# Splitting an output projection into three steps of rows, and joining a short projection, in a hybrid trunk step

## The chip, the cores and the metric

The kernel runs on one core of a Trainium2 chip. The metric is device time in microseconds (us) of that core, the median over several runs. A core has five engines that work side by side: TensorE (PE in the profile; its weight loads are shown apart as PEld), VectorE (DVE), ScalarE (ACT), GpSimd (POOL) and SyncE (SP), which here issues all the DMAs. SBUF is the on-chip memory with 128 partitions, PSUM the small memory into which TensorE writes its results.

## What is computed

One inference step of a layer for 2048 prompt tokens and 128 decode tokens ("samples": 8 sequences of 16 tokens). One input projection feeds three groups of heads, and one output projection joins them:

```python
h = rms_norm(x, norm_g) @ w_in                    # 1024 -> 3654 columns
fox_cols, rwkv_cols, mem_cols = jnp.split(h, ...)
# 6 "fox" heads x 64: causal attention with forget gates (bias on the logits)
# 6 RWKV-7 heads x 64: token shift, decay and learning rate from a small LoRA, a state scan
# 4 memory heads x 64: attention into 256 memory tokens
o = jnp.concatenate([o_f * silu(g_f), o_r * silu(g_r), o_m * silu(g_m)], axis=-1)   # 1024 rows
y = x + o @ w_out
```

For the samples the fox heads attend to 512 cached keys each, the memory heads to 256 cached ones. The mixed row `o` has 1024 entries, which the kernel treats as eight chunks of 128: chunks 0, 1, 2 are the fox heads in pairs, 3, 4, 5 the RWKV heads, 6, 7 the memory heads. The output projection is a sum over these chunks, so it can be made in steps, each adding its chunks to a partial `y`.

## The kernel before

**Two phases.** The first (lines 122 to 943) makes the projections and the RWKV heads, in four rounds of 512 tokens; round 0 carries the 128 sample tokens as well, so it has 640. The second (from 946) makes the fox and memory attention and the output projection. What passes between them goes through DRAM: `q_d`, `k_d`, `v_d`, `mq_d` (token by column), the gates `fg_d`, `mg_d`, the mixed rows `o_d` (column by token), and the partial result `y_d`.

**Projections.** A weight block of up to 256 columns is split into a high and a low part by `wd_load` (line 177), and a product is three matmuls (high x high, high x low, low x high) for each of eight chunks of the 1024 inputs, 24 matmuls in all. `proj_d` (210) gives columns by tokens: the weight is stationary and up to 512 tokens stream. `wide` (735) gives tokens by columns: a tile of 128 tokens is stationary and 256 columns stream, so no transposition is needed for `q`, `k`, `v` and the memory queries. At the head of a round `lora_in` (328) makes 64 LoRA columns and 6 forget-gate columns in one `proj_d` of 70 columns; `forget_cols` (316) turns the 6 back into tokens by columns. The second 128 columns of the memory queries ("m", 128) come out of `pair` (772) and `narrow` (748) as columns by tokens, are copied, and are turned by `turn` (756).

**Attention.** A unit is one pair of heads and one block of 512 queries: 12 fox units (three pairs, four blocks) and 8 memory units. For every tile of 128 keys (`kt`) and each head, `scores` (1144) makes two matmuls into `pS`, ACT makes the exponentials `P` (1153), and the running sum `z` of the exponentials is added up at 1159 and 1161. `ZE = "GGV"` says on which engine: every third key tile from 2 on is VectorE's, the others GpSimd's. `values` (1163) multiplies with the values, four key tiles behind. `sums` (1199) and `out` (1218) scale the result by the reciprocal sums, which come through DRAM, and by the gate, and write it to `o_d`; the fox unit that comes last keeps its result in SBUF. The samples have steps of their own (`sample`, 1226): three pairs of fox heads, two of memory heads.

**Output projection.** `project` (1348) takes a set of chunks and a tile of 128 tokens: it loads the rows of `o_d`, splits them (`oh`, ACT and GpSimd), loads the partial `y` (`xo`, two buffers), makes three matmuls into `py` per chunk and half, adds on VectorE and writes. The weights `W` lie in buffers of the tag `big`, of which there are seven; the samples and the memory heads use the same ones.

**The order.** Every step is put at a place between 0 and 1 on the way through the 12 fox units (`spread`, 1454; the units go with their lengths). The memory units and the first step of the projection (chunks 3, 4, 5, all 17 tiles, onto `x`) lie from 0.02 to 0.35; all samples from 0.35 to 0.6, fox first; then, to 0.8, chunks 6, 7 for tiles 12 to 15, the weights of chunks 0, 1, 2, and the sample tile. Tiles 0 to 11 get chunks 6, 7, 0, 1, 2 in one step (`late`, 1440), four behind each of the last fox units, from 0.8 on. Tiles 12 to 15 get chunks 0, 1 from 0.98 on, and chunk 2 at the very end (`project_last`, 1378). After that `_arrange` (1924) plans all instructions anew: it lists them by engine with costs of its own, ranks them by the place in which they were written and by what lies behind them, and gives each engine one fixed order. So the places are wishes, and the queues are in the order that the plan gives.

Of the kernel before, what the change touches and what calls it, by code (L numbers as in the profile page):

```python
# [30 lines left out]
X0, X3, X1, X2 = 0.02, 0.35, 0.6, 0.8  # L31
# [19 lines left out]
def kernel(ctx: ExitStack, tc: tile.TileContext, I: dict, O: dict):  # L51
# [70 lines left out]
    with ExitStack() as p1:  # L122
# [166 lines left out]
        def shifted(hl, c, m, ci, xk, blocks, it, key, extra=0, tok0=0):  # L289
# [5 lines left out]
            for off, n in blocks:  # L295
                out = proj_d(hl, c, m + extra, xk, off, n)
                if extra:
                    forget_cols(out[64:70, :n], spans(tok0, off, n))
# [17 lines left out]
        def forget_cols(src, where):  # L316
            n = sum(x[1] for x in where)
            sb = sm.tile([128, 512], F32, tag="gth", name="fsb")[64:70, :n]
            S.copy(sb, src)
            pt = pj.tile([128, 512], F32, tag="pj", name="pf")  # L320
            for t in range(n // 128):
                PE.transpose(pt[:, 6 * t:6 * t + 6], sb[:, 128 * t:128 * t + 128], ident[64:70, 64:70])
            for a, m, r0 in where:
                t0, t1, nt = a // 128, r0 // 128, m // 128
                tt(V, fl[:, t1:t1 + nt, :], pt[:, 6 * t0:6 * (t0 + nt)].rearrange("p (t h) -> p t h", h=6),
                   bf_b.unsqueeze(1).to_broadcast([128, nt, 6]), A_)

        def lora_in(hl, xk, blocks, it, tok0):
            xs, xss = shifted(hl, 0, 64, 12, xk, blocks, it, "l", 6, tok0)
# [344 lines left out]
        turned = []  # L674

        def after(*step):

            if turned:
                f, *args = turned.pop()
                f(*args)  # L680
            if step:
                turned.append(step)


# [50 lines left out]
        def wide(parts, xk, nt, t0):  # L735
            hl = wd_load(*columns(parts), src="w_mem" if parts[0][0] in "KV" else "w_in")
            for a in range(0, nt, 2):
                m = min(2, nt - a)
                out = pj.tile([128, 2, 256], F32, tag="pj", name="pjt")
                for t in range(m):  # L740
                    ts_ = slice(128 * (a + t), 128 * (a + t) + 128)
                    for k in range(KC):
                        for x, y in ((0, 0), (0, 1), (1, 0)):
                            mm(out[:, t], xk[k][:, x, ts_], hl[y][k // 4][:, k % 4],
                               start=k == 0 and x + y == 0, stop=k == KC - 1 and x == 1)
                put(out[:, :m], parts, 16 if a == 4 else t0 + a)

        def narrow(hl, c, part, xk, blocks, tok0):

            for off, nb in blocks:  # L750
                out = proj_d(hl, c, 128, xk, off, nb)
                sb = sm.tile([128, 512], F32, tag="gth", name="tsb")[:, :nb]
                S.copy(sb, out[:, :nb])
                after(turn, sb, off, nb, part, tok0)

        def turn(sb, off, nb, part, tok0):
            pt = pj.tile([128, 512], F32, tag="pj", name="ptok")
            for t in range(nb // 128):
                PE.transpose(pt[:, 128 * t:128 * t + 128], sb[:, 128 * t:128 * t + 128], ident)
            for a, m, r0 in spans(tok0, off, nb):  # L760
                put(pt[:, a:a + m].rearrange("p (t c) -> p t c", c=128), [part], r0 // 128)
# [10 lines left out]
        def pair(xk, blocks, tok0, *two):  # L772

            at = lambda w, c: {"f": FG, "g": MG, "m": MQ}[w] + c
            hl = wd_load(*((at(w, c), 128) for w, c in two))
            for j, (w, c) in enumerate(two):
                if w == "m":
                    narrow(hl, 128 * j, (w, c), xk, blocks, tok0)
                else:
                    gate(hl, 128 * j, (fg_d if w == "f" else mg_d)[c:c + 128], xk, blocks, tok0)  # L780

        def constants():
# [3 lines left out]
            ts(V, qg8, qg8, 0.125, None, M, ALU.bypass)  # L786
            mg, mG = (x.rearrange("p a b -> p (a b)") for x in (maskG, I["maskG"]))
# [98 lines left out]
        for it in range(4):  # L886
# [10 lines left out]
            nt, t0 = n // 128, 4 * it  # L897
# [4 lines left out]
                (("m", 128), ("f", 0)), (("f", 128), ("f", 256)), (("g", 0), ("g", 128)))]  # L902
            for p in range(3):
                finish()
                cols = {}
                for two in ((("k", RW + 384, 3), ("r", RW, 0)), (("v", RW + 768, 6), ("g", RG, 9))):
                    hl = wd_load(*((c0 + 128 * p, 128) for _, c0, _ in two))
                    for j, (key, _, ci) in enumerate(two):
                        cols[key] = shifted(hl, 128 * j, 128, ci + p, xk, blocks, it, key)
# [23 lines left out]
        after()  # L933
# [12 lines left out]
    with ExitStack() as p2:  # L946
# [15 lines left out]
        gap = lt.tile([128, 112], F32, tag="gap", name="gap", bufs=1)  # L962
        V.memset(gap[0:1, 0:1], 0.0)
# [174 lines left out]
        def attend(U, q, qb, hp, fox, gsrc, dst):  # L1138
# [79 lines left out]
            def out():  # L1218
                tt(V, R["ob"], R["ob"], R["rb"], M)
# [6 lines left out]
        def sample(fox, hp):  # L1226
# [6 lines left out]
            def load():  # L1233
                m = big("sC")
# [18 lines left out]
            def masked(h):  # L1253
                rr = slice(64 * h, 64 * h + 64)
                D = R["D", h] = big("sD")
# [6 lines left out]
                m = big("sA")[:, 0:512 * nkt]  # L1262
# [6 lines left out]
            def soft(h):  # L1269
# [4 lines left out]
                sb = R["sb"] = R["D", h][:, 640:1280]  # L1274
# [20 lines left out]
            def turn(h):  # L1295
                PT = R["PT", h] = R["D", h][:, 1280:1920].rearrange("p (a b) -> p a b", b=128)
# [51 lines left out]
        def project(W, ks, t, xsrc, dst):  # L1348
# [3 lines left out]
            def load():  # L1352
                ot = lt.tile([128, 5, 128], F32, tag="ot", name="ot", bufs=1)[:, :n]
# [6 lines left out]
                W["o", t] = oh = lt.tile([128, 2, 5, 128], F32R, tag="oh", name="oh")[:, :, :n]  # L1360
# [17 lines left out]
        def project_last(W, held):  # L1378
# [9 lines left out]
            def rows_in(t):  # L1388
                ot = lt.tile([128, 5, 128], F32, tag="ot", name="ot", bufs=1)[:, 0:2]
                ts_ = slice(1536 + 128 * t, 1664 + 128 * t)  # L1390
                SY.dma_start(ot, o_d[0:256, ts_].rearrange("(k p) t -> p k t", p=128))
                ohs[t] = oh = lt.tile([128, 2, 5, 128], F32R, tag="oh", name="oh")[:, :, 0:2]
# [3 lines left out]
            def split():  # L1396
                ohs["held"] = hl = lt.tile([128, 2, 5, 128], F32R, tag="oh", name="oh")[:, :, 0:4]
                src = held["ob"].rearrange("p (t c) -> p t c", t=4)
                S.copy(hl[:, 0], src)
                tt(V, hl[:, 1], src, hl[:, 0].bitcast(F32), SUB)  # L1400

            def half(t, j, last):
                y, js = ys[t // 2][:, t % 2], slice(512 * j, 512 * j + 512)
                oh, own, ks = (ohs["held"], t, (2,)) if last else (ohs[t], 0, (0, 1))
                py = qa.tile([128, 512], F32, tag="pt", bufs=PTB, name="py")
                for k in ks:
                    for a, b in ((0, 0), (0, 1), (1, 0)):
                        mm(py, oh[:, a, own if last else k, :], W[k][:, b, js],
# [646 lines left out]
```

## Time and profile before

| | |
|---|---|
| median of 3 runs | 1762.91 us (1760.62 to 1770.31) |
| profiled execution, its own time | 1764.2 us |
| its span, first to last instruction | 1762.2 us |
| mean granted TensorE clock | 0.971 |
| busy: PE, DVE, ACT, POOL | 1639.0, 1053.2, 727.2, 677.6 us |
| moved by DMA | 302.88 MB, 172 GB/s over the span |

In the profile a row of a group names the line, the engine, the operation, what is written and what is read (buffer numbers left out), the shape and the count, then busy time and mean length of one, then the idle time ahead of them and what ended it. Almost all matmuls share line 58 and almost all tensor operations line 61 (they are helpers), so the tile names tell them apart: `pjd` and `pjt` are projections, `pS` scores, `pm` the products for the row maximum, `po` values, `py` the output projection, `sA` to `sD` the samples' buffers. Some matmul records can be missing from a trace.

### The profile page before, as it was taken

The page shows a single profiled execution, that of the slowest core. Times are in us where ns is not written, and L with a number is a line of the kernel's source. Part 1 is how long each engine was busy: PE and PEld are TensorE (multiplying, and loading weights), DVE is VectorE, ACT ScalarE, POOL GpSimd, SP SyncE. Part 2 cuts the span into 40 slices and gives each one's busy share as a digit, 9 for nine tenths or more (in the row PEclk, how much of TensorE's full clock was granted, in tenths as well). Part 3 has the DMA queues.
Part 4 walks back from the last instruction along what each step waited for, and adds up shares of the span by engine and source line. Part 5 has one row for each costly group of instructions (what it writes and reads, how often), then busy time and mean ns, then how long its engine had stood idle before and what let it go on. Part 6 is the DMA issues. An engine that isn't in the chain of part 4 may idle for free. (4 is left out here: it accounts for less than half of the span.)

```text
span 1762.2 us, 39877 instructions
## 1 busy us (share of the span) xinstructions
PE 1639.0 (93%) x16009; PEld 1277.3 (72%) x16009; DVE 1053.2 (60%) x2448; ACT 727.2 (41%) x1457; POOL 677.6 (38%) x704
## 2 busy tenths in 40 slices
PE   4989999999999999999999999799999888989998
PEld 3989988787887688877787887556666554556766
DVE  7654545572554673444674373589877866796534
ACT  6424252433243433233424243465565534654231
POOL 4554543231322241222133133244665433645252
PEclk8999999999999999999999999899999989999999
DMA  7764745564635655554654645624446653363433
GB/s 219 247 212 146 254 160 187 186 207 127 210 127 170 215 195 169 190 173 134 217 175 133 186 132 169 189 92 160 149 164 204 229 190 129 126 195 132 144 126 108
DMA packets 235319, 302.88 MB, mean 172 GB/s; under 512 B 80644, under 2 KB 185026, under 8 KB 219262
## 3 DMA queue, kind: packets, MB, share of 16 engines
q1 hardware_dynamic: 235134, 300.33, 52.1%
q8 instruction: 126, 2.06, 0.5%
q14 instruction: 59, 0.48, 0.1%
HBM read 210.07 MB, written 90.20 MB: 170 GB/s over the span
## 5 line engine op out<-in xcount | busy, mean ns | idle before, releaser
L58 PE MATMUL pjd<-xk,w 128*128 128x512 f32 (+5 forms) x2280 | 539.0, 376 | 23.1 <-DMA w<-w_d 6.4
L58 PEld LDWEIGHTS pjd<-xk,w 128*128 128x128 f32 (+1 forms) x2280 | 380.2, 189 | 89.0 <-DVE xk L61 9.3
L58 PE MATMUL pjt<-w,xk 128*128 128x256 f32 x2040 | 293.1, 289 | 1.1 <-DVE xsk L64 1.1
L58 PEld LDWEIGHTS pjt<-w,xk 128*128 128x128 f32 x2040 | 265.2, 190 | 11.4 <-issue 4.6
L58 PE MATMUL py<-W,oh 128*128 128x512 f32 x816 | 231.9, 399 | 1.1 <-DVE xo L61 0.6
L1153 ACT ACTIVATE P<-pS,NB 128x512 f32<-128x512 f32 (+1 forms) x240 | 144.4, 624 | 131.0 <-DVE pS L61 64.6
L58 PE MATMUL pS<-Q,K 128*128 128x512 f32 (+1 forms) x480 | 157.8, 405 | 20.1 <-ACT P L1153 12.6
L61 POOL TENSOR_TENSOR z<-z,P 128x512 f32<-128x512 f32 (+3 forms) x120 | 136.2, 1147 | 99.2 <-ACT P L1153 76.8
L58 PEld LDWEIGHTS py<-W,oh 128*128 128x128 f32 x816 | 149.6, 189 | 34.1 <-issue 2.6
L58 PEld LDWEIGHTS pS<-Q,K 128*128 128x128 f32 x480 | 85.8, 196 | 58.2 <-ACT P L1153 32.3
L58 PE MATMUL pm<-K,Q 128*128 128x512 f32 (+3 forms) x240 | 98.6, 430 | 10.0 <-DVE mx L1098 4.6
L1098 DVE TENSOR_REDUCE mx<-pm 128x1 f32<-128x512 f32 x144 | 95.6, 681 | 20.2 <-PE pm L58 19.5
L61 POOL TENSOR_TENSOR nr<-nr,mhalf 128x8 f32<-128x8 f32 (+2 forms) x43 | 62.2, 1448 | 112.4 <-DVE nr L67 103.8
L58 PE MATMUL po<-P,vt 128*64 128x512 f32 (+1 forms) x480 | 98.5, 555 | 0.0
L61 POOL TENSOR_TENSOR w<-wraw,w 128x1024 fp32r<-128x1024 f32 (+1 forms) x34 | 80.9, 2387 | 43.1 <-ACT w L202 43.0
L61 POOL TENSOR_TENSOR oh<-ot,oh 128x384 fp32r<-128x384 f32 (+2 forms) x38 | 43.8, 1153 | 108.4 <-ACT oh L1361 80.6
L61 DVE TENSOR_TENSOR xo<-py,xo 128x512 f32<-128x512 f32 x68 | 45.9, 681 | 54.9 <-PE py L58 54.7
L61 DVE TENSOR_TENSOR ytmp<-yt 64x14 f32<-64x14 f32 (+9 forms) x210 | 55.1, 262 | 37.6 <-DMA yt<-ld 33.2
L58 PEld LDWEIGHTS pm<-K,Q 128*128 128x128 f32 x240 | 47.8, 204 | 39.1 <-DVE mx L1098 14.2
L61 POOL TENSOR_TENSOR z<-P 128x512 f32<-128x512 f32 (+1 forms) x40 | 49.7, 1256 | 68.7 <-ACT P L1153 68.4
L58 PEld LDWEIGHTS po<-P,vt 128*64 128x64 f32 x480 | 33.2, 143 | 56.2 <-issue 54.5
L61 DVE TENSOR_TENSOR z<-z,P 128x512 f32<-128x512 f32 (+3 forms) x72 | 63.0, 880 | 16.6 <-POOL z L61 8.0
(397 smaller groups left out, 2745.8 us busy)
## 6 DMA issues: line engine op xcount, KB each, us to landing
w<-w_d SPq DMA_DIRECT2D x84, 1024.0 KB
w_d<-w SPq DMA_DIRECT2D x28, 1024.0 KB
y_d<-xo SPq DMA_DIRECT2D x21, 512.0 KB
wraw<-in_w_in SPq DMA_DIRECT2D x36, 256.0 KB
xo<-in_x SPq DMA_DIRECT2D x17, 512.0 KB
xo<-y_d SPq DMA_DIRECT2D x17, 512.0 KB
xt<-in_x SPq DMA_DIRECT2D x24, 256.0 KB
xraw<-in_xT SPq DMA_DIRECT2D x24, 256.0 KB
```

Of the source, the lines that this page charges most:

```text
L58: PE.matmul(out, lhsT, rhs, start=start, stop=stop, skip_group_check=True)
L61: e.tensor_tensor(out=out, in0=a, in1=b, op=op)
L1098: V.tensor_reduce(out=to, in_=pm[:, :n], op=MAX, axis=AX.X)
L1153: S.activation(P_[:, c0:], pS[:, c0:], AF.Exp, bias=NB[:, qb, 2 * hp + h, kt:kt + 1] if fox else 0.0)
```

## The change

- The output projection goes in three steps. Chunks 3, 4, 5 stay as they were. Chunks 6, 7, 0 are added for tiles 0 to 15 (6, 7 alone for the sample tile) from 0.37 to 0.68, as a partial `y` in `y_d`. Chunks 1, 2 remain for `late` (from 0.78 on) and for `project_last`, where chunk 1 comes ahead and chunk 2 last. The sample tile gets chunks 0, 1, 2 at 0.9, for which the weights of chunk 0 are loaded a second time.
- The memory heads' samples lie from 0.37 to 0.65 and the fox heads' from 0.66 to 0.9. The memory heads' samples take fewer `big` buffers.
- All running sums are GpSimd's (`ZE = "G"`), and so is the scaling of a unit's result by the reciprocal sums.
- The second 128 columns of the memory queries, the 64 LoRA columns and the 6 forget-gate columns are one block of 198 columns, made as tokens by columns at the head of a round. The 64 LoRA columns are turned back by TensorE (17 tiles in all); the transpositions of the 6 and of the 128 columns go. The remaining gate blocks are paired anew.
- Buffers: 14 instead of 15 for `P`, 8 instead of 7 for `big`, three chunks instead of five in a tile of `o` rows; an unused tile `gap` goes. The split of the last unit's result uses two `P` buffers. The gains of the norms are loaded ahead of the first joined projection.

```diff
-ZE = "GGV"
+ZE = "G"
-PMB, PSB, PB, ZB, GRP, LAG, NKB, BIG, POB, PTB = 2, 2, 15, 2, 4, 1, 4, 7, 1, 3
+PMB, PSB, PB, ZB, GRP, LAG, NKB, BIG, POB, PTB = 2, 2, 14, 2, 4, 1, 4, 8, 1, 3
-X0, X3, X1, X2 = 0.02, 0.35, 0.6, 0.8
+X0, X3, X2 = 0.02, 0.35, 0.78
+MID, S1, S2 = (0.37, 0.68), (0.37, 0.65), (0.66, 0.9)
...
+        def lora_in(sb, blocks, it):
+
+            def turned_(off, n):
+                pt = pj.tile([128, 512], F32, tag="pj", name="plo")
+                for t in range(n // 128):
+                    PE.transpose(pt[0:64, 128 * t:128 * t + 128], sb[:, off // 128 + t, :], ident)
+                return pt
+
+            xs, xss = shifted(turned_, 64, 12, blocks, it, "l")
...
+        def token_major(hl, xk, nt, n):
...
-                            mm(out[:, t], xk[k][:, x, ts_], hl[y][k // 4][:, k % 4],
+                            mm(out[:, t, :n], xk[k][:, x, ts_], hl[y][k // 4][:, k % 4],
...
+        def first_wide(hl, xk, nt, t0):
+
+            sb = sm.tile([128, 512], F32, tag="gth", name="lsb")[:, :64 * nt].rearrange("p (t c) -> p t c", c=64)
+            for a, m, out in token_major(hl, xk, nt, 198):
+                t = 16 if a == 4 else t0 + a
+                S.copy(sb[:, a:a + m], out[:, :, 128:192])
+                tt(V, fl[:, t:t + m, :], out[:, :, 192:198], bf_b.unsqueeze(1).to_broadcast([128, m, 6]), A_)
+                put(out[:, :, 0:128], [("m", 128)], t)
+            return sb
...
-            xk = prep_x(tok0, n, I["x"], I["xT"], V_G, between=lambda: lora.append(wd_load((LORA, 64), (FV + 384, 6))))
-            lora_in(*lora, xk, blocks, it, tok0)
+            xk = prep_x(tok0, n, I["x"], I["xT"], V_G, between=lambda: lora.append(wd_load((MQ + 128, 128), (LORA, 64), (FV + 384, 6))))
+            nt, t0 = n // 128, 4 * it
+            if not it:
+                norm_gains()
+            lsb = first_wide(*lora, xk, nt, t0)
             if not it:
                 constants()
+            lora_in(lsb, blocks, it)
...
-                (("m", 128), ("f", 0)), (("f", 128), ("f", 256)), (("g", 0), ("g", 128)))]
+                (("f", 0), ("f", 128)), (("f", 256), ("g", 0)), (("g", 128),))]
...
-                tt(V, R["ob"], R["ob"], R["rb"], M)
+                tt(G, R["ob"], R["ob"], R["rb"], M)
...
-                D = R["D", h] = big("sD")
+                D = R["D", h] = big("sD") if fox else R["m"][:, 768 + 640 * h:1408 + 640 * h]
...
-                m = big("sB")[:, 0:4 * nk]
+                m = (big("sB") if fox else both[:, 1024:2048])[:, 0:4 * nk]
...
-        for fox, n in ((True, 3), (False, 2)):
-            for hp in range(n):
-                samples += sample(fox, hp)
+        for hp in range(2):
+            samples += sample(False, hp)
+        others = sum((sample(True, hp) for hp in range(3)), [])
...
-        W, wload = out_weights((6, 7, 0, 1, 2))
-        mid = wload[:2]
-        for t in range(12, 16):
-            mid += project(W, (6, 7), t, y_d, yt(t))
-        mid += wload[2:] + project(W, (6, 7, 0, 1, 2), 16, y_d, O["y_s"])
+        W1, mid = out_weights((6, 7, 0))
+        for t in range(16):
+            mid += project(W1, (6, 7, 0), t, y_d, yt(t))
+        mid += project(W1, (6, 7), 16, y_d, yt(16))
+        W, wload = out_weights((1, 2))
+        W2, wlast = out_weights((0,))
 
         def late(t):
-            return project(W, (6, 7, 0, 1, 2), t, y_d, O["y_p"][128 * t:128 * t + 128, :])
+            return project(W, (1, 2), t, y_d, O["y_p"][128 * t:128 * t + 128, :])
...
-        spread(samples, X3, X1, 3)
-        spread(mid, X1, X2, 2)
+        spread(samples, *S1, 3)
+        spread(mid, *MID, 2)
+        spread(wload, MID[1], X2, 2)
+        spread(others, *S2, 3)
+        spread(wlast + project(collections.ChainMap(W2, W), (0, 1, 2), 16, y_d, O["y_s"]), S2[1], S2[1] + 0.03, 3)
```

More of the change, by code (lines that the diff above doesn't have):

```diff
@@ L743, in wide @@
                         for x, y in ((0, 0), (0, 1), (1, 0)):
-                            mm(out[:, t], xk[k][:, x, ts_], hl[y][k // 4][:, k % 4],
+                            mm(out[:, t, :n], xk[k][:, x, ts_], hl[y][k // 4][:, k % 4],
                                start=k == 0 and x + y == 0, stop=k == KC - 1 and x == 1)
[L746 to L761, printed above, removed]
+                yield a, m, out[:, :m]
+        def wide(parts, xk, nt, t0):
+            hl = wd_load(*columns(parts), src="w_mem" if parts[0][0] in "KV" else "w_in")
+            for a, m, out in token_major(hl, xk, nt, 256):
+                put(out, parts, 16 if a == 4 else t0 + a)
+        def first_wide(hl, xk, nt, t0):
[6 more added lines that the diff above has]
+            return sb
         def gate(hl, c, dst, xk, blocks, tok0):
@@ L1396, in split @@
             def split():
[L1397 to L1400, printed above, removed]
+                ohs["held"] = hl = [lp.tile([128, 512], F32R, tag="P", name="hl", bufs=PB) for _ in range(2)]
+                S.copy(hl[0], held["ob"])
+                tt(V, hl[1], held["ob"], hl[0].bitcast(F32), SUB)
             def half(t, j, last):
                 y, js = ys[t // 2][:, t % 2], slice(512 * j, 512 * j + 512)
-                oh, own, ks = (ohs["held"], t, (2,)) if last else (ohs[t], 0, (0, 1))
+                ks = (2,) if last else (1,)
+                oh = [x[:, 128 * t:128 * t + 128] for x in ohs["held"]] if last else [ohs[t][:, a, 0, :] for a in range(2)]
                 py = qa.tile([128, 512], F32, tag="pt", bufs=PTB, name="py")
```

66 lines of the change are left out of this document (19 added, 47 removed).

## The prediction

> **What bounds the kernel now.** I read the page first, then the stages by window, then single tiles by stage, then TensorE's order of time where it is gapless. From the page, the busy shares and the slices:
>
> ```profile
> span 1762.2 us, 39877 instructions
> PE 1639.0 (93%) x16009; PEld 1277.3 (72%) x16009; DVE 1053.2 (60%) x2448; ACT 727.2 (41%) x1457; POOL 677.6 (38%) x704
> ...
> PE   4989999999999999999999999799999888989998
> DVE  7654545572554673444674373589877866796534
> ...
> POOL 4554543231322241222133133244665433645252
> PEclk8999999999999999999999999899999989999999
> ```
>
> TensorE looks full nearly everywhere, but a busy PE counts a matmul from its start to its end, and matmuls overlap; so how full it is has to come from the distance between starts (the pitch). The same engines by stage (columns: stage, length, PE, PEld, DVE, ACT, POOL busy with counts, granted clock, DMA share, GB/s). The projections run to about 1110 us; the rest is attention and output projection:
>
> ```profile
> 44.00:1100.00 1056.00, 1010.29 (x12617) 863.19 (x12617) 551.27 (x1378) 384.26 (x824) 356.93 (x362) 0.99 0.55 180
> ...
> 1144.00:1364.00 220.00, 211.04 (x1000) 137.55 (x1001) 181.00 (x370) 130.77 (x234) 119.95 (x125) 0.97 0.47 154
> 1364.00:1540.00 176.00, 156.77 (x1163) 94.38 (x1161) 131.61 (x321) 89.20 (x173) 76.85 (x84) 0.90 0.50 169
> 1540.00:1628.00 88.00, 79.92 (x360) 51.41 (x359) 74.67 (x156) 43.55 (x74) 44.31 (x45) 0.98 0.49 163
> 1628.00:1762.00 134.00, 129.20 (x582) 93.64 (x580) 58.47 (x97) 34.69 (x58) 46.53 (x39) 0.99 0.37 127
> ```
>
> Call the four last stages A, hole, C and tail. Now the output projection alone (tile py, PE counts in the first bracket) in these four, then the P tiles, whose ACT count is the number of exponentials, my measure of how far attention has come:
>
> ```profile
> 1144.00:1364.00 220.00, 90.91 (x290) 52.30 (x290) 21.83 (x32) 0.97 0.47 154
> 1364.00:1540.00 176.00, 10.66 (x34) 6.17 (x34) 2.73 (x4) 0.90 0.50 169
> 1540.00:1628.00 88.00, 33.70 (x110) 20.18 (x110) 6.70 (x10) 0.98 0.49 163
> 1628.00:1762.00 134.00, 96.61 (x384) 70.97 (x382) 25.41 (x38) 0.99 0.37 127
> ```
>
> ```profile
> 1144.00:1364.00 220.00, 44.32 (x216) 14.19 (x216) 20.91 (x24) 65.91 (x110) 73.72 (x64) 0.97 0.47 154
> 1364.00:1540.00 176.00, 34.82 (x152) 11.21 (x152) 19.94 (x24) 49.38 (x82) 58.21 (x51) 0.90 0.50 169
> 1540.00:1628.00 88.00, 14.90 (x80) 5.42 (x80) 8.91 (x10) 23.86 (x41) 28.45 (x28) 0.98 0.49 163
> 1628.00:1762.00 134.00, 19.36 (x96) 6.35 (x96) 13.26 (x14) 23.94 (x40) 27.17 (x24) 0.99 0.37 127
> ```
>
> The pitches come from gapless runs of one kind in TensorE's order of time (start, length, what):
>
> ```profile
> 89.70 11.17 PE L58 MATMUL pjt<-w,xk 128*128 128x256 f32 x91
> ...
> 597.94 5.00 PE L58 MATMUL pjd<-xk,w 128*70 128x512 f32 x21
> ...
> 1259.80 0.34 PE L58 MATMUL pS<-Q,K 128*128 128x128 f32 x2
> 1259.97 0.45 PE L58 MATMUL pm<-K,Q 128*128 128x512 f32 x1
> ...
> 1403.05 3.65 PE L58 MATMUL po<-P,vt 128*64 128x512 f32 x16
> ```
>
> Less the last matmul's own length (about 0.4 and 0.3 us) that is (5.00-0.4)/20 = 0.230 us at 512 columns and (11.17-0.3)/90 = 0.121 at 256; two of 128 columns, with fresh weights each, fill the 0.17 us to the next row: 0.085. One exponential stands for two score matmuls (0.46), a share of the value matmuls (3.6 us per 8, 0.45) and one max matmul (0.23): 1.14 us of TensorE. With it the work in each stage is: A 110 x 1.14 + 290 x 0.230 = 192 of 220 us (0.87); tail 40 x 1.14 + 384 x 0.230 = 134 of 134 (1.00). For the hole one more term, the decode samples' matmuls (tile sD):
>
> ```profile
> 1364.00:1540.00 176.00, 39.84 (x654) 25.59 (x654) 22.28 (x47) 13.82 (x36) 1.87 (x9) 0.90 0.50 169
> ```
>
> Hole: 82 x 1.14 + 34 x 0.230 + 39.8 = 141 of 176 (0.80); C: 41 x 1.14 + 110 x 0.230 = 72 of 88 (0.82). So the tail is bounded by TensorE alone, while the hole and C lose 51 us, with the clock down to 0.90: the samples and attention there wait on other engines and have little output projection to fill the gaps.
>
> **The change, part by part.** *Output projection in three steps.* The count of py matmuls stays: 816. After the hole's start the old order keeps 34 in the hole, 110 in C, 384 in the tail. In the new one rows 6, 7, 0 are done for all tiles in the middle (300 matmuls), so only rows 1, 2 (144), the last four tiles (48) and the sample tile (18) are left late: 210, against 432 (late 360, last 72) with what belongs to them. I put 200 in the tail and 528-200 = 328 in hole and C. The samples spread: about a third of their 39.8 us (13) falls into the tail. Tail: 40 x 1.14 + 200 x 0.230 + 13 = 105 us at full density, **-29**. Hole and C: 123 x 1.14 + 328 x 0.230 + 27 = 243 us of work in what took 264. The density there is the unknown. At the hole's own 0.80 they take 303 (+39); at A's 0.87, 279 (+15); were A and they at 0.95, 256 (-8) and 202 in A (-18).
>
> A is the nearest row, the same mixture of attention and filler; but DVE is the engine loaded most there (181.00 of 220), and the next part takes a good deal of it away. I take 0.90 for both: hole and C 270 (**+6**), A 213 (**-6**). Together -29; with 2 us for the third weight set (row 0 is loaded and split twice), **-27**, with ends +10 and -55.
>
> *Sums and the scaling moved to GpSimd* (tiles z and ob; min/median/max in ns, then a wait, then groups with mean ns):
>
> ```profile
> L61 POOL TENSOR_TENSOR z<-z,P x120: 452/1280/2248, 1156.7 to 1726.7; 128x512 f32<-128x512 f32 x78, 128x128 f32<-128x128 f32 x18, 128x256 f32<-128x256 f32 x12, 128x384 f32<-128x384 f32 x12
> L61 DVE TENSOR_TENSOR z<-z,P x72: 273/692/1810, 1154.9 to 1725.5; 128x512 f32<-128x512 f32 x48, 128x256 f32<-128x256 f32 x12, 128x384 f32<-128x384 f32 x6, 128x128 f32<-128x128 f32 x6
> ...
> L61 POOL TENSOR_TENSOR ob<-ob,gt x20: 1267/1287/1745, 1174.7 to 1733.4; 128x512 f32<-128x512 f32 x20
> L61 DVE TENSOR_TENSOR ob<-ob,rb x19: 678/837/1561, 1172.1 to 1672.5; 128x512 f32<-128x512 f32 x19
> ```
>
> ```profile
> DVE ob L61 <- DMA rb<-rd: 15.1, 14, 3.0
> ```
>
> ```profile
> L61 DVE TENSOR_TENSOR xo<-py,xo 128x512 f32<-128x512 f32 x68 | 45.9, 681 | 54.9 <-PE py L58 54.7
> L61 POOL TENSOR_TENSOR oh<-ot,oh 128x384 fp32r<-128x384 f32 x17 | 17.7, 1038 | 41.3 <-ACT oh L1361 35.2 <-DMA rb<-rd 3.7 <-issue 2.3
> ```
>
> 72 sums leave DVE (63.0 us by the P rows: 20.91+19.94+8.91+13.26) with 19 scalings (19 x 0.9 = 18); 26 more py additions come (26 x 0.681 = 18): -63 net on DVE. GpSimd gets 48 full sums at 1.28 (61), 24 short ones at about 0.73 (18), 19 scalings at 1.29 (25) and 13 more splits, but narrower ones (+3): +107 on the 288 us of the four stages. In A it goes from 119.95 to about 178 of 213 us (0.83), DVE from 181 to 137. I cost it at nothing, because a sum only gives back a P buffer and TensorE has py matmuls to do meanwhile; without that cover a full sum is 0.6 us later per exponential it holds. A new wait comes with it: the scaling waits for the reciprocals from DMA (15.1 us in all), now in GpSimd's queue; behind it stand the next unit's sums and the o splits that py needs, and ACT waits for the P buffers they hold.
>
> The Trainium skill, "GPSIMD Engine Reference", section 4.1, speaks against this part: two-input elementwise work belongs on VectorE, GpSimd being about twice as slow. The medians agree (1280 against 692); by that price alone, 48 sums at twice 0.692 would be 66 us, not 61, and the sum above would not move.
>
> *More trips of y.* 13 tiles more are read from and written to y_d, 512 KB each way:
>
> ```profile
> xo<-y_d SPq DMA_DIRECT2D x17, 512.0 KB
> ...
> L1221 SPq DMA_DIRECT2D o_d<-ob x19: 319/343/1882, 1176.4 to 1675.5; - x19
> ```
>
> That is 13.6 MB, and with the o rows 42 more issues on SP's queue, 42 x 0.34 = 14 us of it over some 400 us. The DMA engines are half idle there (0.50 and 0.49): nothing, as long as the loads are issued a tile ahead; late, each of the two xo buffers would hold TensorE. P with 14 buffers instead of 15 lets the scores run one exponential less ahead; the eighth big buffer serves the third weight set; the smaller memory samples take fewer of them; the dropped gap tile does nothing: no time for these.
>
> *Joined projection.* Old: per round 24 lora matmuls and 24 for the second half of the memory queries, 512 columns each; 17 + 17 transposes in all. New: 24 of 198 columns per token tile, 17 transposes. Rows: the start of the program, the lora group, the transposes that go:
>
> ```profile
> 0.00:44.00 44.00, 19.95 (x73) 13.94 (x74) 31.25 (x69) 27.30 (x66) 19.55 (x28) 0.84 0.73 218
> ```
>
> ```profile
> L58 PE MATMUL pjd<-xk,w 128*70 128x512 f32 x72 | 23.9, 407 | 0.2
> ```
>
> ```profile
> L759 PE MATMUL ptok<-ident,tsb x17: 270/271/279, 268.7 to 1104.8; 128*128 128x128 f32 x17
> ```
>
> 198 columns lie between 0.085 and 0.121; on the line between, 0.105. Rounds 1 to 3: 48 x 0.230 = 11.0 against 96 x 0.105 = 10.1, -0.9 each (-2.8 to +0.6); the transposes saved there, 12 at 0.085, -1.0. Round 0: 24 x (0.121 + 0.176) = 7.1 of memory query work leaves the full stretch, and in the starved first 44 us 120 x 0.105 = 12.6 replace 7.1. Hidden whole: -7.1; not at all: -1.6; the half megabyte more of weights, at 218 GB/s, can add 2.4. I take -5. The gains' four loads now go ahead of the other constants: under 2 us of SP's queue, inside the same wait for x. Phase sum **-8**, ends +3 and -17.
>
> The Trainium skill, "TensorE: Matmul & The Clock Gate", section LDWEIGHTS, gives P/1.2 ns, 107 for 128 columns, whatever streams; a 198-column matmul could then not go below that. The 0.085 rows disagree; by the rule each of these rounds would save 0.8 instead of 0.9.
>
> The sum is made against the profiled execution: 1764.2 (2.0 around the span of 1762.2) - 8 - 27 = 1729; the median of the runs lies 1.3 lower, so **1728**.
>
> **Rivals.** *Denser still*: if DVE was what held A, A and the middle reach 0.95: -55 + 2 - 8, 1702. For it: 63 us off DVE and a clock back at 1.00. Against: PE's waits name ACT first.
>
> *The filler finds no gaps.* The middle keeps 0.80 because its gaps are chains, not missing work, or the planner already hoists all that dependencies allow: 303 in the middle, A as it was: +39 - 29 + 2 - 8, 1767, no change. For it stand the waits for exponentials and the samples' short matmuls; against it, A, where the same chains ran at 0.87 beside 290 py matmuls:
>
> ```profile
> PEld pS L58 <- ACT P L1153: 35.4, 74, 1.8
> ```
>
> *GpSimd becomes the bound* (slower). It serves its queue in order; where its load must fit a share s, A takes 178/s and the middle 190/s (121 + 69). Break-even with the gains of tail and start is at s = 0.70 (A 254, middle 271: +34 + 7 + 2 - 29 - 8 = +6). The most that 44 us have shown is 29.50, or 0.67:
>
> ```profile
> 1496.00:1540.00 44.00, 41.63 (x296) 24.32 (x295) 31.79 (x64) 29.49 (x55) 29.50 (x27) 0.95 0.37 118
> ```
>
> At 0.67, A 266 and the middle 283: +46 + 19 + 2 - 37, 1793. Against it: there GpSimd was waiting for exponentials, and DVE went to 0.85 and more in other stretches; a sum that is late costs only when 14 P buffers are used up.
>
> **How the numbers follow.** Forecast (0.88 to 0.92 in A and middle; 1712 to 1748) 0.53; denser 0.14; no gaps 0.18; GpSimd 0.12; the rest a start that turns out late, 0.03. A difference of 0.5% (8.8 us) is what a measurement of this kernel can tell from none. Faster: forecast, denser, and a part of the third case, 0.71; same 0.15; slower 0.14. The range 1698 to 1770 takes in the ends down to denser and up to no gaps, and leaves out GpSimd.
>
> **What would show it.** The tail (last 40 exponentials) near 105 us; about 300 py matmuls between A and it, with a clock near 1.00 there; GpSimd near 0.8 and DVE near 0.65 in A; 198-column matmuls near 0.105 apart; the projections' end some 8 us earlier. I am wrong if TensorE's waits there turn to POOL (P buffers, oh), or if the stretch from A's end to the tail grows past 290 us.

## The result, and the profile after

The changed kernel takes 1751.34 us (median of 6 runs, 1738.33 to 1763.43) against 1762.6 us before (6 runs beside them): a ratio of 0.9931, 95% interval 0.9903 to 0.996. That is 11 us less, where 35 were forecast, and inside the range of 1698 to 1770.

The page of the changed kernel, its busy shares and slices:

```profile
span 1761.6 us, 40309 instructions
PE 1644.9 (93%) x16160; PEld 1303.5 (74%) x16160; DVE 1007.7 (57%) x2395; ACT 732.8 (42%) x1476; POOL 773.4 (44%) x814
...
PE   5989999999999999999999999969999899998998
DVE  7663536473526373535484536277765796469735
...
POOL 4563625233203132312223304236678666755655
PEclk9998999999999999999999999969999989999999
```

The load has moved as the change says: DVE 1053 to 1008, POOL 678 to 773. The profiled execution of it (1763.43) is the slowest of its six, so the two profiles are equally long; what differs is where they spend it. A mark that both have is the first operation of the second phase on the forget gates, a scan of 48 rows. DVE's timeline of before, then of after (start, length, what):

```profile
1141.56 1.83 DVE L992 TENSOR_TENSOR_SCAN cl<-one,cl 48x512 f32<-48x512 f32 x1
```

```profile
1174.22 2.01 DVE L975 TENSOR_TENSOR_SCAN cl<-one,cl 48x512 f32<-48x512 f32 x1
```

Windows cut at 100 us and at this scan (columns as in the prediction), before and then after:

```profile
100.00:1141.56 1041.56, 989.22 (x12401) 834.80 (x12399) 540.07 (x1378) 378.21 (x808) 333.39 (x350) 0.99 0.55 177
1141.56:1762.00 620.44, 576.93 (x3100) 376.97 (x3100) 448.19 (x946) 298.22 (x537) 290.03 (x298) 0.96 0.46 154
```

```profile
100.00:1174.22 1074.22, 1009.30 (x12543) 861.77 (x12541) 542.91 (x1401) 381.22 (x814) 331.63 (x355) 0.96 0.53 170
1174.22:1761.00 586.78, 559.23 (x3079) 369.42 (x3079) 396.53 (x865) 300.26 (x545) 384.66 (x399) 0.97 0.56 187
```

By this mark the second phase lost 33 us (620 to 587), a little more than the -27 forecast, and the first phase did not lose 8 us but gained 33: TensorE stands idle 64.9 us of it instead of 52.3 (length less PE), and its clock is 0.96 instead of 0.99. The phases overlap, so the split depends on the mark: the last projection matmul starts at 1145.5 us instead of 1122.4 (23 later, where 8 earlier was forecast), and the first exponential of the attention comes at 1168.1 instead of 1148.0, which would make it 20 us gained and 21 lost. By any of them what has to be explained is not the output projection but the first phase, of which the change touched only the head of each round and the pairing of the gate blocks.

### The profile page after: what moved, and what is told of

Read it like the earlier page. It is cut to its first block, busy times and chain, and to the rows that moved or that the text cites. A ratio compares the mean times of both kernels' runs of the same rounds, so it can differ in the third digit from the quotient of the medians.

```text
span 1761.6 us, 40309 instructions
## 1 busy us (share of the span) xinstructions
PE 1644.9 (93%) x16160; PEld 1303.5 (74%) x16160; DVE 1007.7 (57%) x2395; ACT 732.8 (42%) x1476; POOL 773.4 (44%) x814
## 4 chain that ended last, share of the span: by engine, by line
PE 49%; DMA 12%; DVE 8%; ACT 3%; issue 2%; SPq 2%; POOL 1%; DVEq 0%; POOLq 0%; ACTq 0%
PE pjd L59 9%; PE py L59 9%; PE pjt L59 7%; PE pS L59 6%; PE po L59 5%; PE pm L59 3%; DMA w<-w_d 2%; PE sc L59 1%; DMA sp_d<-spr 1%; DMA inv_d<-yt 1%; DMA rb<-rd 1%; PE sy L59 1%; PE pz L59 1%; PE gr L59 1%; DMA yd<-sp_d 1%
## 5 line engine op out<-in xcount | busy, mean ns | idle before, releaser
L59 PE MATMUL pjd<-xk,w 128*128 128x512 f32 (+2 forms) x2040 | 485.8, 376 | 12.4 <-DMA w<-w_d 6.0
L59 PEld LDWEIGHTS pjd<-xk,w 128*128 128x128 f32 x2040 | 345.5, 192 | 63.8 <-ACT qk L704 7.7
L59 PE MATMUL pjt<-w,xk 128*128 128x256 f32 (+1 forms) x2448 | 364.0, 295 | 5.5 <-DVE xk L62 1.8
L59 PEld LDWEIGHTS pjt<-w,xk 128*128 128x128 f32 x2448 | 331.6, 198 | 20.6 <-issue 4.5
L59 PE MATMUL py<-W,oh 128*128 128x512 f32 x792 | 242.5, 406 | 4.0 <-DVE rb L1177 1.8
L62 POOL TENSOR_TENSOR z<-z,P 128x512 f32<-128x512 f32 (+1 forms) x192 | 207.1, 1102 | 41.6 <-ACT P L1136 37.5
L62 POOL TENSOR_TENSOR nr<-nr,mhalf 128x8 f32<-128x8 f32 (+2 forms) x46 | 62.2, 1352 | 105.8 <-DVE nr L68 99.5
L59 PE MATMUL pm<-K,Q 128*128 128x512 f32 (+2 forms) x240 | 95.7, 423 | 12.5 <-DVE mx L1078 3.8
L62 DVE TENSOR_TENSOR xo<-py,xo 128x512 f32<-128x512 f32 x94 | 64.2, 685 | 61.5 <-PE py L59 57.7
L62 POOL TENSOR_TENSOR w<-wraw,w 128x1024 fp32r<-128x1024 f32 (+2 forms) x34 | 80.8, 2383 | 40.0 <-ACT w L203 35.4
L62 DVE TENSOR_TENSOR ytmp<-yt 64x14 f32<-64x14 f32 (+9 forms) x210 | 53.1, 253 | 30.8 <-DMA yt<-ld 26.1
L704 ACT COPY qk<-pjt 128x512 f32<-128x512 f32 (+2 forms) x56 | 29.1, 530 | 83.2 <-PE pjt L59 74.4
```

The lines of the kernel that those rows point to most:

```text
L59: PE.matmul(out, lhsT, rhs, start=start, stop=stop, skip_group_check=True)
L62: e.tensor_tensor(out=out, in0=a, in1=b, op=op)
L704: S.copy(o_, out)
```

## The experiments

Two theories came out of this reading. *J*: the joined projection itself makes the first phase longer. *P*: it is the plan. The planner orders all instructions anew in every kernel, so the RWKV rounds got another order too, and what an order is worth scatters. A third, *S*, holds that the first phase lost nothing and only the boundary moved. In the table "after" is the changed kernel. All times are set against runs of before beside them on the same chip (medians 1762.6 for the changed kernel, then 1764.8, 1770.46, 1766.05 and 1768.45 for the four groups of experiments), so the ratios are what to compare. "Scan" is the mark above and "rest" is the span behind it, "idle" is TensorE's from 100 us to the scan; these three are of the one profiled execution, and where the order of the first phase is the same (before and the four kernels named pin) the scan still lies anywhere from 1141.6 to 1155.1.

| kernel | median us | ratio (95%) | scan | rest | idle |
|---|---|---|---|---|---|
| before | | 1 | 1141.6 | 620.6 | 52.3 |
| beforeplan | 1778.29 | 1.0059 (1.0028 to 1.0091) | 1145.7 | 620.0 | 49.8 |
| p1only | 1786.21 | 1.0117 (1.0071 to 1.0163) | 1169.1 | 617.2 | 62.2 |
| badorder | 1785.51 | 1.008 (1.0053 to 1.0107) | 1172.5 | 611.5 | 70.3 |
| after | 1751.34 | 0.9931 (0.9903 to 0.996) | 1174.2 | 587.4 | 64.9 |
| afterplan | 1751.44 | 0.9929 (0.9899 to 0.9958) | 1155.7 | 583.0 | 58.3 |
| afterC | 1753.69 | 0.99 (0.9858 to 0.9941) | 1152.7 | 597.9 | 60.1 |
| afterD | 1741.31 | 0.9812 (0.9756 to 0.9868) | 1157.7 | 588.8 | 61.1 |
| p2only | 1745.7 | 0.9898 (0.9869 to 0.9926) | 1162.7 | 592.1 | 60.9 |
| p2plan | 1758.35 | 0.9933 (0.9907 to 0.9959) | 1169.4 | 588.0 | 65.8 |
| p2onlyC | 1764.89 | 0.9968 (0.9943 to 0.9992) | 1159.9 | 599.4 | 60.5 |
| first | 1751.7 | 0.9899 (0.985 to 0.9949) | 1164.4 | 595.2 | 60.5 |
| later | 1747.71 | 0.9875 (0.9829 to 0.9922) | 1153.1 | 593.8 | 52.1 |
| laterplan | 1761.78 | 0.9963 (0.9937 to 0.9988) | 1165.9 | 590.6 | 62.3 |
| pinold | 1733.55 | 0.9829 (0.9808 to 0.985) | 1148.3 | 583.5 | 51.1 |
| pinold_plan | 1733.0 | 0.9823 (0.9804 to 0.9842) | 1144.9 | 586.4 | 49.5 |
| pinold_V | 1749.44 | 0.991 (0.9892 to 0.9928) | 1155.1 | 605.7 | 55.8 |
| pinbefore_G | 1754.36 | 0.9954 (0.9933 to 0.9974) | 1143.6 | 613.4 | 48.3 |

**The two halves, and the planner alone.** The kernel p2only is the change without the joined projection, p1only the joined projection alone:

```diff
 p2only, against the changed kernel
-            lsb = first_wide(*lora, xk, nt, t0)
+            lora_in(*lora, xk, blocks, it, tok0)
...
-                (("f", 0), ("f", 128)), (("f", 256), ("g", 0)), (("g", 128),))]
+                (("m", 128), ("f", 0)), (("f", 128), ("f", 256)), (("g", 0), ("g", 128)))]
```

```diff
 afterplan and beforeplan, against the changed kernel and the kernel before
-_TRIES = ((0.3, 0), (0.45, 0), (0.6, 0))
+_TRIES = ((0.35, 0), (0.5, 0), (0.65, 0))
```

> Before's projections (no joined projection) with the whole of the change behind them: three steps, spread samples, sums and scaling on GpSimd, 14 P buffers. Everything is planned anew. Theory J (the joined projection costs phase 1 some 23 to 32 us, and the second phase gained the 34 us that the two traces show): 1762.6 - 34 = 1729 us, projections end (last projection matmul, start of the forget scan of the second phase) near 1142 us as before. Theory P (any new plan moves phase 1 by up to 20 us, the joined projection itself is worth -8): 1729 plus up to 20 either way, and projections that end elsewhere than at 1142. Theory S (nothing was lost in phase 1, the boundary only moved and the second phase gained 11): 1751.

> Only the joined projection (198 columns, new pairs of gate blocks, gains loaded ahead), the rest as before. Theory J: 1762.6 + 23 to 32 = 1786 to 1795 us, second phase 640 us long. Theory P: 1755 plus or minus 20. Theory S: 1755, second phase about 620.

> The changed kernel, same instructions, but the planner starts from three other weights (0.35, 0.5, 0.65 for 0.3, 0.45, 0.6), so every engine has another order. Theory J: within 5 us of 1751. Theory P: another time by 10 us or more, and the start of the second phase moves by as much (1174 in the profile of after).

> The kernel before, same instructions, with the same three other weights in the planner. Theory J: within 5 us of 1763. Theory P: another time by 10 us or more, with the start of the second phase moved from 1142.

Theory S falls at once: the rest is 620.6, 620.0 and 617.2 with the old second phase and 583.0 to 592.1 with the new one, and p1only takes 1786 us where S expected 1755. Between J and P the four decide less cleanly. The joined form costs 21 us beside the old second phase, in J's range, but 6 beside the new one; the two halves do not add up. The changed kernel under other weights takes 1751.44 us, the same as under its own, which is what J expected and not P. But the kernel before, with nothing changed but the planner's weights, loses 0.6%, some 10 us, as P expected. And in p2only the scan is at 1162.7, not at 1142, although not one instruction of the projections differs from before.

**Where in the first phase?** The first and second RWKV scans of round 0 start later with the joined head, so the start was a suspect. Two kernels make the old columns in round 0 or in the others:

```diff
 later: JOIN = (1, 2, 3); first: JOIN = (0,); laterplan: as later, with the other weights
+            if it in JOIN:
                 lsb = first_wide(*lora, xk, nt, t0)
...
+            else:
+                lora_in(None, blocks, it, (lora[0], xk, tok0))
```

> The changed kernel, but round 0 makes its LoRA, forget-gate and memory-query columns in the old way; joined only in rounds 1 to 3. The scans that start each RWKV part stand, as a mean over three kernels each, 5.5 us (first scan) and 11 us (second scan) later with the joined start than with the old one, and 8 to 16 us later from there on. Theory start (the joined block delays the start of round 0 and nothing else): 1742 to 1746 us, the second scan near 160 us. Theory rounds (rounds 1 to 3 lose it too, through fewer dense matmuls that could keep the clock up): 1750 us or more, the second scan near 160 but the second phase starting as late as with the whole change. Theory plan (the fixed order that comes out scatters by 7 us or more and hides both): no such pattern, and the next kernel differs by 7 us or more.

> The same as the kernel before it in this call (joined only in rounds 1 to 3), planned from three other weights. Theory start: 1742 to 1746 us. Theory rounds: 1750 or more. Theory plan: off by 7 us or more from its twin.

> The changed kernel with the joined block only in round 0, the old form in rounds 1 to 3. Theory start: 1751 to 1756 us, second scan near 171 us. Theory rounds: 1746. Theory plan: anything from 1740 to 1760.

> The kernel with the old projections and all the rest of the change, planned from three other weights. Theory start and theory rounds: within 4 us of the 1746 that its twin took. Theory plan: off by 7 us or more; and if it comes out at 1751 or above, the 6 us between its twin and the changed kernel are luck.

(In both hybrids four weight blocks have to be split twice, since the pairs differ between rounds.) Twins that differ only in the plan lie 0.9% apart (later, laterplan) and 0.35% (p2only, p2plan), which is as much as anything that the form of the projections shows. The place cannot be found in this way; theory P fits best so far.

**The order held.** To take the scatter out, the planner was made to keep, on every engine, the order that the first phase has in the kernel before, and to plan only the second:

```diff
+            mine = _PIN[e][turn[e]] if turn[e] < len(_PIN[e]) else -1
             for x in xs:
+                if x < _PINNED and x != mine:
+                    continue
                 r = possible(x) if x <= base + _WINDOW else None
```

```diff
 pinold_V, against pinold (pinbefore_G makes the opposite edit in the kernel before)
-ZE = "G"
+ZE = "GGV"
-                tt(G, R["ob"], R["ob"], R["rb"], M)
+                tt(V, R["ob"], R["ob"], R["rb"], M)
```

> The old projections and all the rest of the change (three steps, spread samples, sums and scaling on GpSimd), but every engine's order within the first phase is fixed to the very order of the kernel before; only the second phase is planned anew. Theory plan (the first phase grew by 11 to 32 us in the other kernels because each new plan of it came out worse than that of before, whatever form the projections had): the forget scan of the second phase starts at 1142 us give or take 4, what follows it takes 590 as in the seven kernels with the new second phase (583 to 595), in all 29 us less than before. Theory reach (the new second phase itself holds the first one back, through the queues or the buffers they share): the scan starts at 1155 to 1169 and the kernel is 10 to 18 us below before, as its freely planned twins.

> The same with the fixed first phase, the second phase planned from three other weights. Theory plan: within 5 us of its twin, since the scatter of the plans sits in the first phase (the second phases of seven kernels lie within 12 us of each other). If the second phase scatters as much as the first did, 7 us or more off.

> The same with the fixed first phase, but every third running sum and the scaling by the reciprocal sums back on VectorE. Theory three steps (the gain of the second phase comes from the placing of the output projection; the move to GpSimd is worth nothing, as the prediction costed it): within 5 us of the twin with all sums on GpSimd. Theory relief (VectorE held the stage up, the move is half of the gain): 10 to 20 us more than the twin.

> The kernel before with its own order of the first phase fixed, and of the change only the sums and the scaling on GpSimd. Theory three steps: as before within 5 us. Theory relief: 10 to 15 us below before. Theory GpSimd too slow by itself: above before by 5 us or more.

With the old order of the first phase the same change of the second takes 1733.55 and 1733.0 us, 1.7% to 1.8% below before and below the changed kernel as well, with the scan at 1148.3 and 1144.9 (1142, give or take 4, was expected). The two plans of the second phase differ by 0.5 us. Of all kernels only afterD, below, has as low a ratio, from four widely spread runs. The same instructions in three free plans (p2only, p2plan, p2onlyC) have 0.9898, 0.9933 and 0.9968, that is 13, 19 and 25 us more. The windows of pinold:

```profile
100.00:1148.30 1048.30, 997.20 (x12423) 841.11 (x12421) 541.24 (x1391) 379.38 (x811) 333.27 (x350) 0.98 0.55 176
1148.30:1731.00 582.70, 557.32 (x3086) 369.95 (x3086) 398.16 (x869) 299.12 (x548) 384.50 (x402) 0.97 0.56 189
```

The idle time is back at 51.1 and the second phase at 583. Here the second phase can be laid beside that of before stage by stage, cut at the same exponentials as the prediction's stages (272, 163, 81 and 40 still to come), all engines and then the output projection alone:

```profile
1146.90:1360.20 213.30, 207.47 (x993) 137.33 (x994) 156.39 (x324) 129.86 (x234) 155.44 (x163) 0.97 0.48 159
1360.20:1535.10 174.90, 166.21 (x894) 113.26 (x893) 114.49 (x259) 82.78 (x153) 119.11 (x121) 0.97 0.61 203
1535.10:1629.00 93.90, 89.19 (x663) 57.95 (x662) 77.93 (x186) 51.86 (x99) 55.34 (x66) 0.98 0.67 219
1629.00:1731.80 102.80, 95.05 (x543) 61.70 (x541) 50.75 (x102) 35.78 (x67) 55.24 (x55) 0.98 0.57 198
```

```profile
1146.90:1360.20 213.30, 92.01 (x294) 53.52 (x295) 21.67 (x32) 0.97 0.48 159
1360.20:1535.10 174.90, 85.39 (x277) 50.89 (x276) 21.19 (x31) 0.97 0.61 203
1535.10:1629.00 93.90, 21.53 (x67) 11.90 (x66) 6.16 (x9) 0.98 0.67 219
1629.00:1731.80 102.80, 55.01 (x181) 34.00 (x180) 25.34 (x38) 0.98 0.57 198
```

The output projection of before, cut in the same way:

```profile
1148.00:1362.80 214.80, 90.12 (x289) 52.23 (x290) 21.83 (x32) 0.98 0.46 152
1362.80:1539.80 177.00, 11.24 (x36) 6.23 (x35) 2.73 (x4) 0.90 0.50 170
1539.80:1632.30 92.50, 36.95 (x121) 22.24 (x121) 8.07 (x12) 0.98 0.48 159
1632.30:1762.20 129.90, 93.56 (x372) 68.91 (x371) 24.04 (x36) 0.99 0.38 128
```

The middle took 344 matmuls of the output projection, where before has 157, in no more time (268.8 us for 269.5), and the tail is down to 102.8 from 129.9.

The move to GpSimd, which the prediction costed at nothing, is a part of it. Without it pinold_V stands at 0.991, so 0.8% or 14 us go with it; alone, in the kernel before, it brings 0.46%, 8 us (pinbefore_G). The three steps with the old sums are worth 16 us, so the two together bring 31, more than the 24 that they bring apart. The hole and C of pinold_V, cut at the same exponentials:

```profile
1375.90:1556.50 180.60, 172.41 (x908) 115.16 (x907) 131.32 (x290) 85.32 (x158) 88.47 (x92) 0.97 0.61 200
1556.50:1659.20 102.70, 95.26 (x661) 60.87 (x660) 85.94 (x201) 50.81 (x97) 42.14 (x50) 0.92 0.60 198
```

They take 283 us instead of 269, while A (214.4) and the tail (101.6) do not differ from pinold's. So three steps with the sums where they were win 28 us in the tail and give half of it back in the middle, where the samples and the additions of `py` meet on DVE. That the relief of DVE there is what lets the middle absorb the work is a reading of these rows and was not tested by itself: the profiled execution of pinold_V is 13 us above its median, so the 14 us rest on the runs, not on these two rows, and beside the old steps (pinbefore_G, one execution) it is A that is shorter, 209.3 for 214.8, and the middle hardly, 266.8 for 269.5.

**The order alone, and more plans.** The kernel badorder is the kernel before, every instruction of it, with the first phase held to the order of p2plan. The others are the changed kernel and p2only under further weights:

```diff
 afterC and p2onlyC (afterD: 0.4, 0.55, 0.7)
-_TRIES = ((0.3, 0), (0.45, 0), (0.6, 0))
+_TRIES = ((0.25, 0), (0.4, 0), (0.55, 0))
```

> The kernel before, every instruction of it, with one thing changed: the order of the first phase is fixed to that of the freely planned kernel with old projections that came out slowest (1758 us, where the same instructions in before's order took 1733). The second phase is planned anew. Theory plan (the order alone sets it): some 25 us above before, 1785 to 1795, the forget scan near 1165, about 620 us behind it. Theory reach (that order was slow only beside the new second phase): within 5 us of before.

> The changed kernel, a third plan (weights 0.25, 0.4, 0.55). The old form with the same second phase took 0.9898 and 0.9933 of before in two free plans, the joined form 0.9931 and 0.9929. Theory neutral (the joined form itself is worth nothing that can be told beside the plans): the mean of four joined plans within 0.3% of that of three old ones. Theory loss (it costs some 10 us, seen at the second scan of round 0): the joined plans lie 0.5% above the old ones. Theory gain (it is worth the 8 us of the prediction): 0.4% below them.

> The old form of the projections with the new second phase, a third plan (weights 0.25, 0.4, 0.55). To be set against the joined plans as said there: by the plans so far 0.985 to 0.998 of before.

> The changed kernel, a fourth plan (weights 0.4, 0.55, 0.7). As for the third: 0.985 to 0.998 of before.

An order taken from elsewhere makes the kernel before 0.8% slower by itself (1785.51 against 1768.45 beside it, 17 us; 25 were expected, so a part of p2plan's disadvantage is not the order itself, or is scatter). Its window of the first phase:

```profile
100.00:1172.50 1072.50, 1002.20 (x12444) 846.18 (x12443) 553.65 (x1397) 384.13 (x813) 336.88 (x352) 0.98 0.54 172
```

TensorE idles 70.3 us in it, 18 more than before, with the same matmuls. That settles the sign of theory P: the order alone does this. (In the profile the rest is 9 us shorter than in before, the first phase 31 longer.)

What the joined form itself is worth: four plans of the changed kernel have a mean of 0.9893 (0.9812 to 0.9931), three plans of the old form with the same second phase 0.9933 (0.9898 to 0.9968). The difference is -0.4%, -7 us, just what theory gain expected, but with a standard error of 6 from the scatter of the plans; it hangs on afterD, which fell below the 0.985 to 0.998 that was expected of it. Beside the old second phase its one plan, p1only, was 0.7% above the mean of before, beforeplan and badorder. So a gain as forecast, nothing, and a small loss are all still possible; only the 33 us of the first profile are excluded as its price. The joined form was not tried in before's order, since an order cannot be kept as it is where the weights are paired otherwise; what it is worth in a good order stays open.

## Why the prediction was wrong, and where it was right

*The step that failed* is the one that was not in the sum. "Phase sum -8" priced the instructions that the joined projection adds and removes, and let the rest of the first phase stand as it was in the profile. But `_arrange` plans it all anew, and the sum was made against one particular order. Against pinold, three free plans of the very same instructions cost 13, 19 and 25 us. In their profiles the scan comes 12 to 21 us later than in pinold and the rest is 5 to 16 longer, so most of the term, not all, lies in the first phase. With it the sum reads -31 (pinold) + 19 - 7 = -19 for the mean of the changed kernel's plans, which is 0.9893. This is no check, since the 19 and the 7 are differences of the same means. The plan that was predicted, at 0.9931, is the poorest of the four, by luck. The forecast would have needed a term of about +19 with a spread of 7 either way, and a range and chances to match. A part of it may be chance: before's order is the best of the five in which these instructions were timed, and a new draw is more often worse than the best one.

*Output projection, -27: right, with the move to GpSimd in it.* Held to the same first phase the stages of before and pinold are A 214.8 and 213.3, hole and C 269.5 and 268.8, tail 129.9 and 102.8 (cut at the same exponentials). Forecast were -6, +6 and -29; measured -1.5, -0.7 and -27. The density assumed for the middle was 0.90; by the prediction's measure it is (123 x 1.14 + 344 x 0.230 + 27) / 268.8 = 0.92. The clock there is 0.97 and 0.98, where near 1.00 was forecast and the hole had 0.90. Three slips in the prediction's sums change nothing: A at 0.90 is -7 and not -6, 19 scalings at 0.9 are 17 us and not 18, and GpSimd breaks even at a share of 0.71.

*GpSimd at nothing: wrong in the attribution.* It is worth 14 us here. The prediction did not price it, but chose 0.90 because it would relieve DVE, so the gain stood in the other term. It was looked for in A and the middle alike, and in pinold it shows in the middle; GpSimd's load in A was put at 178 us and is 155 (0.73 of 213, where 0.83 was expected). *GpSimd as the bound* is refuted: in one stretch of the changed kernel it runs at 38.50 of 44 us, over the break-even, beside a full TensorE at full clock, and the waits of the second phase name it only at the end of the list (the window; then PE's waits from the scan on):

```profile
1320.00:1364.00 44.00, 43.25 (x200) 26.68 (x199) 25.53 (x54) 26.21 (x44) 38.50 (x35) 1.00 0.55 179
```

```profile
PE pS L59 <- ACT P L1136: 4.6, 8, 1.1
...
PE pm L59 <- POOL K L992: 0.7, 1, 0.7
```

*Filler finds no gaps* is refuted by 344 matmuls in the middle at no extra time; *denser still* by A, which did not move.

*Joined projection, -8: open, and by its parts too large.* The pitch of 198 columns was put at 0.105 by interpolation. TensorE's timeline of the changed kernel in round 3:

```profile
872.52 5.83 PE L59 MATMUL pjt<-w,xk 128*128 128x198 f32 x50
```

Less a last matmul of 0.3 that is 5.5 / 49 = 0.112, so rounds 1 to 3 save 48 x 0.230 - 96 x 0.112 = 0.3 each, not 0.9. The Trainium skill, "TensorE: Matmul & The Clock Gate", section LDWEIGHTS, with its 107 ns per load was a little nearer to the measured 112 than the line between my two rows (105). And the starved start hides less than I took. TensorE's timeline of before and of after, the first RWKV projection with 384 columns:

```profile
49.44 10.79 PE L58 MATMUL pjd<-xk,w 128*128 128x384 f32 x68 [1.35 <-DVE xsk L64]
```

```profile
55.10 13.27 PE L59 MATMUL pjd<-xk,w 128*128 128x384 f32 x85 [1.05 <-ACT qk L704]
```

It comes 5.7 us later, against the 7.1 us of memory query work that is by then done: -1.4, the case "not at all" (-1.6), instead of -5. Nor is that this plan's bad luck: in the six kernels with the joined start this matmul comes at 55.1 to 60.6 us, in the twelve others at 49.3 to 53.1. Term by term the joined form is worth -1.4 - 3 x 0.3 - 1.0 = -3, if nothing else changes.

## What to carry to other kernels

Where a planner orders everything anew, a local edit is measured together with a new order of all the rest; price that as a term of its own, by timing a few plans of the unchanged kernel first. Hold the order of the part that isn't meant to change: for the change without the joined projection that showed -31 us where three free plans showed -6 to -18. And when work is moved into a stretch to fill it, look at which engine serves the filler there: with the sums left on VectorE, which also makes the additions of `py`, 14 us of the gain were missing.

## What the runs showed of the hardware that was not expected

A short stall of TensorE can cost more than its length. The recorded clock changes only in steps of 3.41 us, between 1.00 and 0.50. Windows of the changed kernel cut at these steps, in rounds 0 and 2:

```profile
114.73:118.14 3.41, 0.82 (x6) 0.43 (x4) 3.34 (x3) 2.20 (x4) 3.37 (x2) 1.00 0.05 20
118.14:121.56 3.42, 3.42 (x16) 3.42 (x17) 2.44 (x5) 0.45 (x1) 2.04 (x2) 0.50 0.08 9
```

```profile
763.27:766.68 3.41, 2.28 (x53) 1.55 (x52) 1.56 (x5) 2.17 (x6) 0.18 (x1) 1.00 0.53 208
766.68:770.10 3.42, 3.40 (x39) 2.50 (x39) 1.14 (x4) 1.58 (x4) 0.18 (x1) 0.50 0.86 298
```

TensorE was idle 2.6 us of the one step and only 1.1 of the other, whose busy part was mostly matmuls of 32 and of 2 columns; both times the next step, fully loaded again, ran at half clock and lost up to 1.7 us (half of the step). Idle time alone does not decide it: a later step of the same kernel with 1.86 us idle was followed by full clock.

```profile
121.56:124.97 3.41, 1.55 (x13) 1.35 (x12) 0.00 (x0) 0.00 (x0) 0.91 (x1) 1.00 0.30 41
124.97:128.39 3.42, 2.07 (x133) 1.90 (x133) 1.24 (x3) 0.85 (x2) 1.42 (x2) 1.00 0.93 294
```

So an order that stalls a little more can pay twice: the first phase of after has 12.6 us more idle time than that of before, and of full clock it misses (1 - 0.962) x 1074 = 41 us instead of (1 - 0.986) x 1042 = 15 (the mean of the recorded clock over the window), a part of them in time in which TensorE stood idle anyway. The same account fits the orders of the old projections: in the ten kernels that have them the stretch from 100 us to the scan is 1042 to 1072 us long, but less the idle time and the missing clock 968 to 982. So more than half of what a poorer order costs is TensorE standing idle or at half clock. That the stalls are what lowers the clock was only argued from these rows; no run changed the clock alone. The Trainium skill, "TensorE: Matmul & The Clock Gate", section "Why this matters for your kernels", advises "No PE-idle gaps >~3µs between matmul bursts"; here 1.1 us idle in a step was enough where small matmuls filled the rest.
